# Start of a hybrid decoder trunk: the input is scaled per chunk, the time steps come from the normalised input, and the residual is added by products with the identity

## The chip, the cores and the metric

The kernel runs on one core of a Trainium2 chip. The metric is the device time of one execution in microseconds, the median of the runs. Before the change it is 2892.61 us (2892.17 to 2893.71, three runs).

The engines that matter here: PE (TensorE) multiplies matrices and transposes, DVE (VectorE) and ACT (ScalarE) work elementwise, POOL (GpSimd) works elementwise and issues a few transfers, SP (SyncE) issues most transfers. Each engine works through its own list of instructions in order and waits where an operand is not ready.

## The reference, cut to what matters

A decoder trunk over 1040 tokens (16 learned meta tokens, then 1024 input tokens) of width 1024: a state-space mixer (SSD) and a gated FFN, then attention and a second FFN. All inputs and outputs are float32. The part the change touches is the way into the first mixer and the way out of it.

```python
h = concatenate([meta_tokens, x])                       # 1040 x 1024
u = h * rsqrt(mean(h*h, -1) + 1e-6) * ssd_norm          # _rmsnorm
z, xbc, dt_raw = split(u @ w_in, [2048, 2048 + 3072])   # dt_raw: 32 columns
xbc = silu(causal_conv4(xbc))
dt = softplus(dt_raw + dt_bias);  a = -exp(a_log)
...                                                     # scan over chunks, gate, group norm: hg
h = h + hg @ w_out
```

## The kernel before, in words

**Layout.** Activations lie transposed: 128 features on the partitions, tokens along the free axis, in eight rows (`KD` = 8) of 1040 tokens. Tokens go in three tiles `TT` of 348, 348 and 344. The input comes in nine chunks `CH` of 116 tokens (the last 112), tokens on partitions; three chunks make one tile.

**Products.** A product in nearly full float32 is made of three fp32r products (`mm3`, lines 190 to 195): both operands are split into a high and a low part (`uh`/`ul`, `wh`/`wl`). `parts` (line 295) makes `uh` on ACT (line 303) and `ul` on DVE (line 304); `load_w` (line 171) loads a weight block, makes `wh` on ACT (line 180) and `wl` on POOL (line 98). A plain float32 product is one call and shows as two PE instructions in the trace.

**The way in (`load_x`, lines 327 to 398).** Two steps for each tile j. `stream(j)`: the sum of squares of each chunk (DVE for the chunks in `SQD`, ACT for the others, line 366), then for each of the eight feature blocks three transposes of the raw chunks on PE (`xT`, line 371), a copy into the row `h` (line 374 or 376) and a plain float32 product with the 32 time-step columns of the weights (`dtr`, line 377); then the factors of the tile (`token_rstd`, lines 244 to 250). `scaled(j)`: the three chunks are multiplied by their factors on DVE (line 388), transposed again (`xr`, line 393) and split by `parts`. The rows `h` are stored to the DRAM tensor `h0_d` (line 379) for the residual. All nine chunk loads are issued at the start, the odd chunks on SP's queue, the even ones on ACT's own list, ahead of ACT's other work.

**The mixer.** `mixer` runs `load_x`, then `dt_path` (the softplus of the time steps and their cumulated sums; it multiplies `dtr` by the factors `r9` first), then `in_group(0)`: six blocks of projections (`pj`, 24 products for each tile), with convolution on ACT and DVE. From the first `cb` product (lines 665 and 666) on, the order on PE, DVE, ACT and POOL is fixed by the program (`manual_schedule`) up to the end of the mixer; outside of it a scheduler chooses the order. The last projections of the mixer are interleaved with `split_y` (lines 807 to 815), which scales and splits the first group's gated rows for the output projection: per tile four times DVE, ACT, DVE.

**The way out (`out_proj`, lines 817 to 836).** The groups g = 0, 1, 2 of the output projection run here; the fourth is in `enter_ffn`. For each g and each output block f (eight), `accumulate` (line 424) makes for each of the three token tiles 12 products into one of five PSUM banks (`cycle` over two `mm`, two `lg`, one `ex`) and DVE adds the bank to the row `h[f]` (line 431). With g = 0 the row `h[f]` is first fetched from `h0_d` (line 419).

Of the kernel before, what the change touches and what calls it, by code (L numbers as in the profile page):

```python
# [69 lines left out]
ORD = ((0, 0), (1, 0), (0, 1), (1, 1), (0, 2), (1, 2))  # L70
# [30 lines left out]
class Trunk:  # L101
    def __init__(self, ctx, tc, a):
        self.tc, self.nc, self.a = tc, tc.nc, a
        nc = self.nc
        self.cp = ctx.enter_context(tc.tile_pool(name="cp", bufs=1))
        self.qp = ctx.enter_context(tc.tile_pool(name="qp", bufs=NQ))
        self.tmps = ctx.enter_context(tc.tile_pool(name="up", bufs=8))
        self.wp = ctx.enter_context(tc.tile_pool(name="wp", bufs=3))
        self.mp = ctx.enter_context(tc.tile_pool(name="mp", bufs=2, space=bass.MemoryType.PSUM))
        self.sp = ctx.enter_context(tc.tile_pool(name="sp", bufs=SMB, space=bass.MemoryType.PSUM))  # L110
        self.dp = ctx.enter_context(tc.tile_pool(name="dp", bufs=1, space=bass.MemoryType.DRAM))
        self.n = 0
        self.open = []
        self.consts()
# [56 lines left out]
    def load_w(self, src, n, gain=None, out=None):  # L171
# [8 lines left out]
        nc.scalar.activation(wh[:, :n], w32[:, :n], AF.Copy)  # L180
# [9 lines left out]
    def mm3(self, out, wh, wl, uh, ul, first, last, joins=False, tie=None):  # L190
# [4 lines left out]
        mm(out, wl, uh, start=False, stop=last, skip_group_check=joins)  # L195
# [41 lines left out]
    def token_rstd(self, ss, m, k, eps=EPS, y=None, src=None):  # L237
# [6 lines left out]
        nc.vector.tensor_scalar(ss[:m, :k], (ss if src is None else src)[:m, :k], 1.0 / D, eps, op0=ALU.mult, op1=ALU.add)  # L244
        nc.scalar.activation(y[:m, :k], ss[:m, :k], AF.Ln)
        nc.scalar.activation(y[:m, :k], y[:m, :k], AF.Exp, scale=-0.5)
# [48 lines left out]
    def parts(self, t, u, s0, n, g, eng=None):  # L295
# [6 lines left out]
        else:  # L302
            nc.scalar.activation(h, t, AF.Copy, scale=g)
            nc.vector.scalar_tensor_tensor(l, t, g, h.bitcast(F32), op0=ALU.mult, op1=ALU.subtract)
# [22 lines left out]
    def load_x(self, pool, mx):  # L327
# [5 lines left out]
        wdt = self.wp.tile([P, 1024], F32, tag="w32", name="wdt")  # L333
        self.ln_exp()
        d = self.dp.tile([KD, P, L], F32, tag="h0_d", name="h0_d")
        r9 = mx.tile([P, 3, 3], F32, tag="r9", name="r9")
        dt = self.ex("dtr")
        xs = []
        for c, (t0, n) in enumerate(CH):
# [4 lines left out]
            else:  # L344
                self.by_rows(nc.sync if c % 2 else nc.scalar, xt[:n, :], a["x"][t0 - META : t0 - META + n, :], n)
            if c == 0:
                nc.sync.dma_start(wdt[:, : KD * H], a["w_dt"])
                v = wdt[:, : KD * H].rearrange("p (k h) -> p k h", k=KD)
                nc.gpsimd.tensor_tensor(v, v, self.par("ssd_norm", 0, KD).unsqueeze(2).to_broadcast([P, KD, H]), op=ALU.mult)
# [4 lines left out]
        hs = [self.Q("h") for _ in range(KD)]  # L354

        def stream(j):
            s0, nn = TT[j]
            x3 = xs[3 * j : 3 * j + 3]
            for i in range(3):
                c = 3 * j + i  # L360
                n = CH[c][1]
                t = self.wp.tile([P, D], F32, tag="wl", name=self.nm("junk"))
                if c in SQD:
                    nc.vector.scalar_tensor_tensor(t[:n, :], x3[i][:n, :], 1.0, x3[i][:n, :], op0=ALU.mult, op1=ALU.mult, accum_out=ss[:n, c : c + 1])
                else:
                    nc.scalar.activation(t[:n, :], x3[i][:n, :], AF.Square, accum_out=ss[:n, c : c + 1])
            for k in range(KD):
                ps = self.lg("xT")
                for i in range(3):
                    n = CH[3 * j + i][1]  # L370
                    nc.tensor.transpose(ps[:, i * CB : i * CB + n], x3[i][:n, k * P : k * P + P], self.ident[:n, :n])
                h = hs[k][:, s0 : s0 + nn]
                if k % 2:
                    nc.scalar.activation(h, ps[:, :nn], AF.Copy)
                else:
                    nc.vector.tensor_copy(h, ps[:, :nn])
                nc.tensor.matmul(dt[j * H : j * H + H, :nn], wdt[:, k * H : k * H + H], h, start=k == 0, stop=k == KD - 1)
                if j == 2:
                    nc.sync.dma_start(d[k], hs[k][:, :L])
            self.token_rstd(ss[:, 3 * j : 3 * j + 3], CB, 3, y=r9[:, :, j])  # L380

        def scaled(j):
            s0, nn = TT[j]
            x3 = xs[3 * j : 3 * j + 3]
            for i, t in enumerate(x3):
                n = CH[3 * j + i][1]
                r = r9[:n, i : i + 1, j]
                nc.vector.tensor_scalar(t[:n, :], t[:n, :], r, None, op0=ALU.mult)
            for k in range(KD):
                ps = self.sm("xr")  # L390
                for i in range(3):
                    n = CH[3 * j + i][1]
                    nc.tensor.transpose(ps[:, i * CB : i * CB + n], x3[i][:n, k * P : k * P + P], self.ident[:n, :n])
                self.parts(ps[:, :nn], u[k], s0, nn, self.par("ssd_norm", k))

        for step, j in ORD:
            (scaled if step else stream)(j)
        return d, u, dt, r9
# [35 lines left out]
    def dt_path(self, ps, r9, cp):  # L434
# [3 lines left out]
        heads = cp.tile([P, 2, H], F32, tag="heads", name="heads")  # L438
        nc.gpsimd.dma_start(heads.rearrange("p i h -> p (i h)"), a["heads"].to_broadcast([P, 2 * H]))
        aneg = heads[:, 1]  # L440
        self.tc.keep_in_program_order(nc.scalar.activation(aneg, aneg, AF.Exp))
        nc.vector.tensor_scalar(aneg, aneg, -1.0, None, op0=ALU.mult)
# [17 lines left out]
        tt(v3, pv[R].rearrange("p (c h) -> p c h", h=H), r9[:CB].rearrange("p i j -> p (i j)").unsqueeze(2).to_broadcast([CB, 9, H]), op=ALU.mult)  # L460
        tt(v3, v3, bias, op=ALU.add)
# [41 lines left out]
    def in_block(self, u, col, cv, out):  # L503
# [3 lines left out]
        def tile(w, j):  # L507
# [4 lines left out]
            self.open.append(lambda: nc.scalar.activation(t, t, AF.Silu))  # L512
# [84 lines left out]
    def settle(self):  # L597

        todo, self.open = self.open, []
# [3 lines left out]
    def stream(self, blocks, w0=None):  # L603
# [11 lines left out]
        for n in range(3 * len(todo)):  # L615
            i, j = divmod(n, 3)
            if j == 0:
                if i + 1 < len(todo):
                    w.append(self.load_w(todo[i + 1][0], D))
                cur = w.pop(0)  # L620
            if n in calls:
# [97 lines left out]
    def mixer(self, mx):  # L719


        with self.tc.tile_pool(name="start", bufs=3) as pool:
            hd, u, *dt = self.load_x(pool, mx)
            dt = self.dt_path(*dt, mx)
        with self.tc.tile_pool(name="ssd", bufs=3) as pool:
            yd, rows = [None] * 4, [[] for _ in range(4)]
# [19 lines left out]
            for n, _ in enumerate(self.stream(into(0))):  # L746
# [51 lines left out]
        return hd, rows[3][:4], yd, list(zip(y0[1], y0[0]))  # L798
# [18 lines left out]
    def out_proj(self, hd, y3, yd, ops, pool):  # L817
# [3 lines left out]
        banks = cycle((self.mm, self.lg, self.ex, self.mm, self.lg))  # L821
        for g in range(3):
# [920 lines left out]
    def run(self, ctx):  # L1743
        tc = self.tc
        with tc.tile_pool(name="mx", bufs=1) as mx:
            hd, y3, yd, y0 = self.mixer(mx)
        self.rp = ctx.enter_context(tc.tile_pool(name="rp", bufs=1))
        with tc.tile_pool(name="ff0", bufs=2) as pool:
            d, *forms = self.out_proj(hd, y3, yd, y0, pool)
# [81 lines left out]
```

## Time and profile before

| | |
|---|---|
| median of three runs | 2892.61 us |
| the profiled execution: its time, and the span from its first to its last instruction | 2892.33 us, 2890.5 us |
| DVE busy, ACT busy, POOL busy (share of the span) | 73%, 56%, 56% |
| first product of the projections (`pj`) | at 32.78 us |
| first `cb` product (the scan begins) | at 131.18 us |
| last product of the mixer, first of the output projection | at 645.29 and 645.45 us |

How to read it: a row of the timeline gives the start and the duration in microseconds, the engine, the line, the operation, output and inputs, and the number of instructions merged into it; in brackets stands how long the engine was idle before and what ended that. PE's instructions overlap: a product lasts about 0.32 us, but the next one starts 0.16 us later. So the cost of PE work is read from the distance of the starts. A row of the windows gives for a stretch of time its length, the busy time of each engine with its number of instructions, then the granted TensorE clock, the share of the DMA engines and GB/s.

### The profile page before, as it was taken

Reading aid. Unit: us, or ns where it says so; the run is one execution under the profiler, and the core shown is the slowest. Engines: PE = TensorE matmul, PEld = TensorE weight load, DVE = VectorE, ACT = ScalarE, POOL = GpSimd, SP = SyncE. Lnnn points to the kernel's source line nnn. Section 1 sums busy time; section 2 is a strip of 40 time slices with the busy share of each in tenths; the row PEclk is TensorE's granted clock in tenths of the full one; section 3 lists DMA queues with packets and bytes.
Section 4 is the critical chain, followed back from the end, with each engine's and each line's share of the span. In section 5 each row is a group of like instructions: output and inputs, shape, how many; then the busy total and the mean of one; then the engine's idle time right before and its main releaser. Section 6 shows DMA issues by size and latency. Waiting matters only on the chain. (4 is left out here: it accounts for less than half of the span.)

```text
span 2890.5 us, 58592 instructions
## 1 busy us (share of the span) xinstructions
PE 2834.6 (98%) x21835; PEld 2701.9 (93%) x21835; DVE 2096.3 (73%) x4044; ACT 1628.0 (56%) x3392; POOL 1610.4 (56%) x2430
## 2 busy tenths in 40 slices
PE   7999999999999999999999999999999999999998
PEld 4999999999999999999999999999798999999888
DVE  5676666668387667666886888888749776767776
ACT  4455544544265656565335888888736565555433
POOL 2265555552429888858743222222363888885882
PEclk9999999999999999999999999999999999999999
DMA  5233333343213222244132222222332222225331
GB/s 168 75 107 95 117 94 117 114 156 135 81 60 97 81 81 76 81 161 164 52 114 78 57 68 66 62 63 54 134 117 74 81 76 79 81 81 183 110 102 66
DMA packets 128265, 278.70 MB, mean 96 GB/s; under 512 B 14787, under 2 KB 58828, under 8 KB 127980
## 3 DMA queue, kind: packets, MB, share of 16 engines
q1 hardware_dynamic: 122028, 261.70, 28.7%
q10 hardware_dynamic: 4112, 6.56, 0.7%
q0 software_dynamic: 1840, 6.70, 0.6%
q8 instruction: 172, 2.82, 0.4%
q14 instruction: 113, 0.93, 0.1%
HBM read 204.63 MB, written 55.36 MB: 90 GB/s over the span
## 5 line engine op out<-in xcount | busy, mean ns | idle before, releaser
L98 POOL TENSOR_TENSOR wl<-w,wh 128x256 fp32r<-128x256 f32 x768 | 682.0, 918 | 377.3 <-ACT wh L180 299.8
L193 PE MATMUL pj<-uh,wh 128*128 128x348 f32 (+2 forms) x1536 | 500.0, 326 | 2.7 <-DVE qs L1469 1.9
L194 PE MATMUL pj<-ul,wh 128*128 128x348 f32 (+2 forms) x1536 | 494.7, 322 | 0.0
L195 PE MATMUL pj<-uh,wl 128*128 128x348 f32 (+2 forms) x1536 | 491.5, 320 | 0.0
L193 PE MATMUL p<-bh,fh 128*128 128x262 f32 (+1 forms) x1408 | 400.4, 285 | 5.5 <-DVE p L1118 5.5
L195 PE MATMUL p<-bh,fl 128*128 128x262 f32 (+1 forms) x1408 | 400.1, 284 | 1.9 <-POOL fl L98 1.9
L194 PE MATMUL p<-bl,fh 128*128 128x262 f32 (+1 forms) x1408 | 398.7, 283 | 0.0
L98 POOL TENSOR_TENSOR fl<-x,fh 128x256 fp32r<-128x256 f32 x352 | 265.6, 786 | 191.9 <-ACT fh L1055 161.5
L193 PE MATMUL p<-bh,wh 128*128 128x262 f32 (+1 forms) x1040 | 295.7, 284 | 1.5 <-ACT ft L1115 1.5
L194 PE MATMUL p<-bl,wh 128*128 128x262 f32 (+1 forms) x1040 | 295.8, 284 | 1.2 <-DVE bl L979 1.2
L195 PE MATMUL p<-bh,wl 128*128 128x262 f32 (+1 forms) x1040 | 295.0, 284 | 0.0
L193 PEld LDWEIGHTS pj<-uh,wh 128*128 128x128 f32 x1536 | 288.3, 188 | 5.0 <-issue 1.9
L194 PEld LDWEIGHTS pj<-ul,wh 128*128 128x128 f32 x1536 | 288.9, 188 | 1.1
L195 PEld LDWEIGHTS pj<-uh,wl 128*128 128x128 f32 x1536 | 288.6, 188 | 0.6 <-issue 0.6
L323 DVE SCALAR_TENSOR_TENSOR c<-p,params,c 128x260 f32<-128x260 f32 (+1 forms) x528 | 248.5, 480 | 53.3 <-ACT c L320 46.7
L193 PEld LDWEIGHTS p<-bh,fh 128*128 128x128 f32 x1408 | 267.1, 190 | 6.3 <-DVE p L1118 5.9
L195 PEld LDWEIGHTS p<-bh,fl 128*128 128x128 f32 x1408 | 267.0, 190 | 2.8 <-POOL fl L98 2.5
L194 PEld LDWEIGHTS p<-bl,fh 128*128 128x128 f32 x1408 | 267.5, 190 | 0.1
L1115 ACT ACTIVATE ft<-p 128x262 f32<-128x262 f32 (+1 forms) x352 | 132.5, 382 | 175.0 <-DVE p L1118 111.2
L195 PE MATMUL acc<-gh,wl 128*128 128x260 f32 (+1 forms) x672 | 213.5, 320 | 2.8 <-POOL wl L98 2.6
L193 PE MATMUL acc<-gh,wh 128*128 128x260 f32 (+1 forms) x672 | 210.9, 320 | 3.1 <-DVE h L1279 3.1
L194 PE MATMUL acc<-gl,wh 128*128 128x260 f32 (+1 forms) x672 | 213.9, 319 | 0.0
(332 smaller groups left out, 7898.9 us busy)
## 6 DMA issues: line engine op xcount, KB each, us to landing
w<-in_w_up SPq DMA_DIRECT2D x88, 512.0 KB
w<-in_w_down SPq DMA_DIRECT2D x44, 512.0 KB
w<-in_w_in SPq DMA_DIRECT2D x40, 512.0 KB
E<-ea_d SPq DMA_DIRECT2D x32, 464.0 KB
D<-acs_d SPq DMA_DIRECT2D x32, 420.5 KB
g<-c SPq DMA_DIRECT2D x88, 130.0 KB
g<-c SPq DMA_DIRECT2D x88, 128.0 KB
b<-g SPq DMA_DIRECT2D x16, 520.0 KB
```

Of the source, the lines that this page charges most:

```text
L98: eng.tensor_tensor(out[:, c], x[:, c], y[:, c], op=op)
L193: self.behind(mm(out, wh, uh, start=first, stop=False, skip_group_check=joins), tie, "behind the sums of squares")
L194: mm(out, wh, ul, start=False, stop=False, skip_group_check=joins)
L195: mm(out, wl, uh, start=False, stop=last, skip_group_check=joins)
L323: ins = nc.vector.scalar_tensor_tensor(out, ps[:, o + i : o + i + n], wcol(i), out, op0=ALU.mult, op1=ALU.add)
L1115: nc.scalar.activation(s[:, :N], ps[:, :N], AF.Copy)
```

## The change

Three things.

- **The input is scaled as its chunks land.** The first three chunk loads are issued ahead (chunks 0 and 2 on ACT's list, all others on SP's queue), then the first weight block and the time-step columns, then the other six chunks. Factors are made for two chunks and then for the third of a tile; a chunk is scaled on DVE, on ACT, or half on each. Only the scaled chunks are transposed, once. The squares of the next tile stand between the splits of this one, and ties without a semaphore (`behind`) fix places in the lists.
- **The time steps come from the normalised input.** The 32 columns are split into a high and a low part and laid into zero-padded tiles `wd`, so that a 96-column operand puts the tile's result at its own 32 partitions. `dtr` is now an `mm3` product with `uh`/`ul`: 24 of them, 72 products. They stand behind the projections of the first block for each tile. `dt_path` no longer multiplies by the factors.
- **The residual is added by products.** The rows `h` and the tensor `h0_d` are gone. In `out_proj` with g = 0, `load_rows` loads a column block of the raw input (128 tokens by 128 features, eight pieces, 512 bytes each) and the 16 transposed meta tokens from a small DRAM tensor. The three tiles of a block f are summed first; then `add_rows` adds the input with eleven plain float32 products against the identity (one for the meta tokens, two chunks split at tile borders), and DVE copies the three banks to `h[f]`. The next block starts behind them.

```diff
@@ load_x
+        for c in range(3):
+            load(c)
+        w32 = self.wp.tile([P, 1024], F32, tag="w32", name="w32_0")
+        nc.sync.dma_start(w32, first)
...
+        nc.sync.dma_start(wdt, a["w_dt"])
+        for c in range(3, 9):
+            load(c)
...
+        def transposed(j, ks):
...
+                    t = nc.tensor.transpose(ps[:, i * CB : i * CB + n], x[:n, k * P : k * P + P], self.ident[:n, :n])
+                    if j:
+                        self.behind(t, self.last_mm, "behind the products in front")
+                made[j, k] = self.parts(ps[:, :nn], u[k], s0, nn, self.par("ssd_norm", k))
+
+        def tile(j):
+            a, b, c = range(3 * j, 3 * j + 3)
+            if j == 0:
+                for x in (a, b, c):
+                    square(x, None)
+            factors(j, 0, 2)
+            scale(a, [(nc.vector, 0, D)])
+            factors(j, 2, 1)
+            scale(b, [(nc.scalar if j else nc.vector, 0, D)], None if j else self.first_factor)
...
+            scale(c, [(nc.vector, 0, D // 2), (nc.scalar, D // 2, D)])
+            transposed(j, range(KD // 2))
+            if j < 2:
+                hi, lo = made[j, KD // 2 - 1]
+                square(a + 3, hi)
+                square(b + 3, lo)
+            transposed(j, range(KD // 2, KD))
+            if j < 2:
+                square(c + 3, made[j, KD - 1][0])
...
+        def steps():
+            tile(0)
...
+            yield
+            for j in range(3):
...
+                for k in range(KD):
+                    w = slice(2 * H + G * k - H * j, 2 * H + G * k - H * j + G)
+                    self.mm3(dt[:G, :n], wd[0][:, w], wd[1][:, w], u[k][0][:, c], u[k][1][:, c], j == k == 0, j == 2 and k == KD - 1, tie=self.last_mm)
+                if j < 2:
+                    tile(j + 1)
...
+                yield
@@ add_rows (new)
+            for c in range(SEQ // P):
+                c0 = META + c * P
+                a, b = max(c0, s0), min(c0 + P, s0 + n)
+                if a < b:
+                    own.append((ps[:, a - s0 : b - s0], t[:, c * P : c * P + P], self.ident[:, a - c0 : b - c0]))
+            for i, (out, lhs, rhs) in enumerate(own):
+                ins = mm(out, lhs, rhs, start=False, stop=i == len(own) - 1, skip_group_check=True)
+                self.behind(ins, self.last_mm, "behind the block's products")
+                self.last_mm = ins
+        for (s0, n), ps in zip(TT, banks):
+            self.nc.vector.tensor_copy(t[:, HB + s0 : HB + s0 + n], ps[:, :n])
@@ mixer
+            u, dt, heads, w0, front = self.load_x(pool, mx, self.a["w_in"][DI // P])
+            dt = self.dt_path(dt, heads, mx)
+            next(front)
+            rows = [[] for _ in range(4)]
+            group = self.stream(self.in_group(u, 0, rows[0]), w0, True)
+            for _ in range(3):
+                next(group)
+                next(front)
@@ out_proj
-                    h[f] = self.fetch(hd[f], "h", front=HB)
+                    h[f] = self.load_rows(f)
+                    sums = []
+                    for s0, n in TT:
+                        ps = next(banks)("acc")
+                        for i, (hi, lo) in enumerate(ops):
+                            c = slice(i * P, i * P + P)
+                            self.mm3(ps[:, :n], w[0][:, c], w[1][:, c], hi[:, s0 : s0 + n], lo[:, s0 : s0 + n], i == 0, False, joins=True, tie=tie if i == 0 else None)
+                        sums.append(ps)
+                    self.add_rows(h[f], sums)
+                    tie = self.last_mm
+                    continue
```

The lists of instructions show three places.

ACT's list at the start, before. `x_108`, `x_117`, `x_123`, `x_129`, `x_135` are the even chunks 0 to 8, `junk` is what a sum of squares leaves:

```order
L405 DMA x_108<-in_x 96x1024
L405 DMA x_108<-in_x 4x1024
L405 DMA x_117<-in_x 112x1024
L405 DMA x_117<-in_x 4x1024
L405 DMA x_123<-in_x 112x1024
L405 DMA x_123<-in_x 4x1024
L405 DMA x_129<-in_x 112x1024
L405 DMA x_129<-in_x 4x1024
L405 DMA x_135<-in_x 112x1024
L366 ACTIVATE junk_177,ss_101<-x_108 116x1024
```

And now, where `x_106` and `x_113` are chunks 0 and 2, `mT` the transposed meta tokens and `r` the factors:

```order
L494 DMA x_106<-in_x 96x1024
L494 DMA x_106<-in_x 4x1024
L494 DMA x_113<-in_x 112x1024
L494 DMA x_113<-in_x 4x1024
L375 ACTIVATE junk_190,ss_101<-x_106 116x1024
L431 ACTIVATE mT_186<-mT_177 128x128
L245 ACTIVATE r_104<-ss_101 116x2
L246 ACTIVATE r_104<-r_104 116x2
L375 ACTIVATE junk_194,ss_101<-x_113 116x1024
L245 ACTIVATE r_104<-ss_101 116x1
```

Five of nine chunk loads stood ahead of ACT's first square; now two chunks' loads do, and the square of chunk 2 stands behind the factors of chunks 0 and 1.

DVE's list at the start, now (`x_110` is chunk 1, `tb` a help tile of the factors). Before, the three scalings stood behind all factors of the tile and behind copies of `h`:

```order
L373 SCALAR_TENSOR_TENSOR junk_192,ss_101<-x_110 116x1024
L244 TENSOR_SCALAR ss_101<-ss_101 116x2
L247 TENSOR_TENSOR tb_196<-r_104 116x2
L248 TENSOR_TENSOR tb_196<-tb_196,ss_101 116x2
L249 TENSOR_SCALAR tb_196<-tb_196 116x2
L250 TENSOR_TENSOR r_104<-r_104,tb_196 116x2
L390 TENSOR_SCALAR x_106<-x_106,r_104 116x1024
L244 TENSOR_SCALAR ss_101<-ss_101 116x1
L390 TENSOR_SCALAR x_110<-x_110,r_104 116x1024
```

Then the factors of chunk 2 and its half scaling follow: nothing but this chain stands on DVE ahead of the first split.

PE's list where the output projection begins, before. `acc_6871` is block 0, tile 0; `acc_6885` block 0, tile 1; `acc_6937` block 1, tile 1; `acc_6923` block 1, tile 0:

```order
L195 MATMUL acc_6871<-yh_6669,wl_6864 128x348
L193 MATMUL acc_6885<-yh_6666,wh_6863 128x348
L193 MATMUL acc_6937<-yh_6666,wh_6915 128x348
L194 MATMUL acc_6885<-y_6484,wh_6863 128x348
L195 MATMUL acc_6885<-yh_6666,wl_6864 128x348
L194 MATMUL acc_6937<-y_6484,wh_6915 128x348
L195 MATMUL acc_6937<-yh_6666,wl_6916 128x348
L193 MATMUL acc_6923<-yh_6666,wh_6915 128x348
```

And now, from the end of block 0, tile 2 (`acc_6852`) to the first product of block 1 (`acc_6890`); `ms` are sums of squares of the last gate group, `h_6823` the loaded input:

```order
L195 MATMUL acc_6852<-yh_6624,wl_6819 128x344
L482 MATMUL acc_6826<-h_6823,ident 128x16
L482 MATMUL acc_6826<-ident,h_6823 128x128 x2
L482 MATMUL acc_6826<-ident,h_6823 128x76
L482 MATMUL acc_6839<-ident,h_6823 128x52
L226 MATMUL ms_6780<-z_6224,ones 128x348
L482 MATMUL acc_6839<-ident,h_6823 128x128 x2
L226 MATMUL ms_6794<-z_6261,ones 128x344
L482 MATMUL acc_6839<-ident,h_6823 128x40
L482 MATMUL acc_6852<-ident,h_6823 128x88
L482 MATMUL acc_6852<-ident,h_6823 128x128 x2
L193 MATMUL acc_6890<-yh_6621,wh_6882 128x348
```

Before, PE took blocks 0, 1 and 2 in turns, whichever token tile was ready; now block 1 begins only when all three tiles of block 0 and its eleven identity products are through.

More of the change, by code (lines that the diff above doesn't have):

```diff
@@ L382, in scaled @@
[L382 to L394, printed above, removed]
@@ L396, in load_x, with square @@
-        for step, j in ORD:
-            (scaled if step else stream)(j)
-        return d, u, dt, r9
+        G = 3 * H
+        wd = [self.Q("wd", F32R) for _ in range(2)]
+        for t in wd:
+            nc.gpsimd.memset(t.bitcast(F32), 0.0)
+        taps = [t[:, 2 * H : 2 * H + KD * G].rearrange("p (k h) -> p k h", h=G)[:, :, :H] for t in wd]
+        made = {}
+        def square(c, tie):
+            n = CH[c][1]
+            t = self.wp.tile([P, D], F32, tag="wl", name=self.nm("junk"))
+            x, acc = xs[c][:n, :], ss[:n, c : c + 1]
+            if c in SQD:
+                ins = nc.vector.scalar_tensor_tensor(t[:n, :], x, 1.0, x, op0=ALU.mult, op1=ALU.mult, accum_out=acc)
+            else:
+                ins = nc.scalar.activation(t[:n, :], x, AF.Square, accum_out=acc)
+            self.behind(ins, tie, "behind the tile in front")
@@ L601, in settle, with stream @@
             f()
-    def stream(self, blocks, w0=None):
+    def stream(self, blocks, w0=None, late=False):
         calls = {}
@@ L797, in mixer @@
                     pass
[L798 removed]
+        return rows[3][:4], yd, list(zip(y0[1], y0[0]))
     def fetch_y(self, d):
```

137 lines of the change are left out of this document (79 added, 58 removed).

## The prediction

> **What bounds the kernel now.** I read the page first, then the windows of the mixer, then the timeline at the two places that the change touches: the start and the beginning of the output projection.
>
> ```profile
> span 2890.5 us, 58592 instructions
> PE 2834.6 (98%) x21835; PEld 2701.9 (93%) x21835; DVE 2096.3 (73%) x4044; ACT 1628.0 (56%) x3392; POOL 1610.4 (56%) x2430
> 131.00:645.30 514.30, 511.52 (x3845) 478.17 (x3844) 342.86 (x820) 267.51 (x393) 293.78 (x398) 1.00 0.37 109
> ```
>
> PE is busy 98% of the span. In the third row, from the first `cb` product to the last product of the mixer (length, then busy time of PE, weight loads, DVE, ACT, POOL), PE works 511.52 of 514.30 us at clock 1.00. The change leaves PE's list of that stretch as it is, so whatever the front gains or loses reaches 645.3 nearly whole, and whatever PE pays after it stands in the span. I therefore count PE time at the two ends and every wait of PE there.
>
> ```profile
> 0.84 14.41 ACTq L405 DMA_DIRECT2D x<-in_x  x9
> 11.35 1.01 PE L371 MATMUL xT<-ident,x 116*128 116x116 f32 x4 [4.95 <-DMA x<-in_x]
> 12.64 1.22 DVE L364 SCALAR_TENSOR_TENSOR junk<-x 116x1024 f32<-116x1024 f32 x1
> 15.36 1.06 ACT L366 ACTIVATE junk<-x 116x1024 f32<-116x1024 f32 x1 [13.27 <-DMA x<-in_x]
> 17.58 0.17 DVE L244 TENSOR_SCALAR ss<-ss 116x3 f32<-116x3 f32 x1 [0.41 <-ACT junk L366]
> 18.83 0.19 ACT L245 ACTIVATE r<-ss 116x3 f32<-116x3 f32 x1
> 19.05 0.21 ACT L246 ACTIVATE r<-r 116x3 f32<-116x3 f32 x1
> 19.29 0.16 DVE L247 TENSOR_TENSOR tb<-r 116x3 f32<-116x3 f32 x1 [1.55 <-ACT r L246]
> 26.55 3.56 DVE L388 TENSOR_SCALAR x<-x,r 116x1024 f32<-116x1024 f32 x3
> 28.72 0.83 PE L393 MATMUL xr<-ident,x 116*128 116x116 f32 x6
> 32.78 0.40 PE L193 MATMUL pj<-uh,wh 128*128 128x352 f32 x1
> 131.18 0.27 PE L665 MATMUL cb<-ident,xbc 128*116 128x128 f32 x1
> ```
>
> The front: chunks 0 and 1 are there at 11.35 (what PE's 4.95 us wait ends on), but ACT issues loads until 15.25 and squares only at 15.36, and the scalings wait until 26.55 behind the copies of `h`. From 28.6 to 131.0 PE works on, first partly cold.
>
> **The front: what PE sheds.**
>
> ```profile
> 33.25 0.77 PE L377 MATMUL dtr<-h,wdt 128*32 128x348 f32 x2
> 33.96 0.52 PE L371 MATMUL xT<-ident,x 116*128 116x116 f32 x3
> 34.31 0.46 PE L393 MATMUL xr<-ident,x 116*128 116x116 f32 x3
> 34.54 0.41 PE L194 MATMUL pj<-ul,wh 128*128 128x352 f32 x1
> 130.85 0.32 PE L194 MATMUL pj<-ul,wh 128*128 128x352 f32 x1
> 131.01 0.33 PE L195 MATMUL pj<-uh,wl 128*128 128x352 f32 x1
> ```
>
> By the distance of starts a `dtr` pair costs 33.96-33.25, less queueing some 0.67; a group of `xT` 0.35; a `pj` 0.16. By the lists, 8 of 24 `dtr` and 10 of 24 `xT` groups are behind PE at 28.6. Of the 102.4 us up to 131.0, 16×0.67 = 10.7 are `dtr`, 14×0.35 = 4.9 `xT`; 86.8 are common to both kernels (456 `pj` = 73.0, 24 `xr` groups at some 0.3 = 7.4, about 1.5 of small work, which leaves 4.9 of waits).
>
> **The front: when PE starts now.** Chunks 0 and 1 at about 11.0; square 1.22, its handoff and the small operation of line 244 to 12.5; Ln and Exp (0.19, 0.21) with handoffs to 13.0; four small DVE operations of 0.16 to 13.8; scaling, 3.56/3 = 1.19 at most (a scaling is 0.93 in the mean, below) to 14.8; line 244 and the second scaling to 15.9; four small ones to 16.7; half a scaling: first complete `xr` group at 17.1, first `pj` near 18. Bounds for the start are 16 (no handoff waits) and 19 (scalings all at 1.19, and chunk 2 late).
>
> **The front: what PE takes on.** 72 `dtr` products at 0.16 = 11.5. And each tile now is paced by its splits:
>
> ```profile
> L303 ACT ACTIVATE uh<-xr,params 128x348 fp32r<-128x348 f32 x16 | 8.3, 548 | 8.2 <-PE xr L393 8.2
> L304 DVE SCALAR_TENSOR_TENSOR ul<-xr,params,uh 128x348 fp32r<-128x348 f32 x16 | 8.8, 572 | 3.3 <-ACT uh L303 3.3
> L388 DVE TENSOR_SCALAR x<-x,r 116x1024 f32<-116x1024 f32 x8 | 7.2, 932 | 1.8 <-PE xT L371 1.8
> ```
>
> Eight splits (4.6), one square (1.2), a scaling (0.9) and the factors (1.0) make 7.7 on DVE; PE has 24 products and 8 groups of transposes, 6.3, beside it: 1.4 of wait for each tile, 4.2. With 2.5 for cold products at the start and 0.7 of handoffs that is 7.4, of which 4.9 stand in the common part: +2.5 (bounds -3, if squares and scalings hide wholly, and +7, if tiles 1 and 2 wait once more for their factors). First `cb`: 17.1 + 86.8 + 11.5 + 2.5 = **117.9**, a gain of **13.1** (bounds 8.5 and 16.5; 20.5 if PE never waited). `dt_path` keeps 123 `pj`, 19.6 us, between its sums and the first `cb`, and hides there.
>
> **The output projection: identity products.**
>
> ```profile
> 131.29 0.36 PE L666 MATMUL cb<-xbc,xbc 128*116 128x116 f32 x2
> 131.49 0.60 PE L669 MATMUL px<-ident,xbc 128*116 128x128 f32 x4
> 131.84 0.41 PE L193 MATMUL pj<-uh,wh 128*128 128x352 f32 x1
> 662.67 1.32 PE L226 MATMUL ms<-z,ones 128*128 128x348 f32 x4
> ```
>
> The nearest row is a plain float32 product of 116 columns: 131.49-131.29 = 0.20, 1.72 ns a column. A block's eleven cover 1040 columns: 1.79, and 0.26 for short ones whose weight load shows: 2.05, times eight **16.4**. From below: a transpose against the identity takes (131.84-131.49)/4 = 0.088 for 128 columns, 0.72 a block, 5.7 in all; from above, line 226 at 1.82 ns a column and every weight load bare, 20.
>
> **The output projection: a new stall.**
>
> ```profile
> 645.29 0.32 PE L195 MATMUL pj<-uh,wl 128*128 128x344 f32 x1
> 645.45 0.32 PE L193 MATMUL acc<-yh,wh 128*128 128x348 f32 x1
> 648.82 0.42 PE L193 MATMUL acc<-yh,wh 128*128 128x348 f32 x1 [0.37 <-DVE h L431]
> 658.11 0.52 DVE L815 TENSOR_TENSOR y<-t,yh 128x344 fp32r<-128x344 f32 x1
> 659.67 0.52 DVE L815 TENSOR_TENSOR y<-t,yh 128x344 fp32r<-128x344 f32 x1 [0.56 <-ACT yh L814]
> 694.33 0.32 PE L193 MATMUL acc<-yh,wh 128*128 128x348 f32 x1
> ```
>
> `split_y` paces by 1.57 us (658.11 to 659.67) through DVE, ACT, DVE, and ends at 660.2. Before, PE filled that time with blocks 1 and 2 on the tiles at hand. Now it may not: after tile 0 (1.9) it gets three products per 1.57. The chain doesn't get faster: the adds of line 431 that go stood in its gaps. In old time block 0 ends at 660.2 + 0.47 (last three products) + 2.05 + 1.28 (two `ms` that the list puts in between, by the row of line 226) = 664.0; without waits at 645.45 + 36×0.159 (the distance of starts there) + 2.05 + 1.28 = 654.5. Of the 9.5 some 1.5 is not new: short waits that the old order had (0.37 shown) and slow single products after them. **8.0**, at least 7.3 if the chain gains half a step, at most 9.5.
>
> Does the stall also cool the clock?
>
> ```profile
> 852.81 0.39 PE L193 MATMUL p<-bh,fh 128*128 128x262 f32 x1 [1.86 <-DVE p L1118]
> 854.00:856.00 2.00, 2.00 (x11) 2.00 (x11) 2.00 (x7) 2.00 (x7) 0.00 (x0) 0.50 0.00 0
> 856.00:858.00 2.00, 2.00 (x14) 2.00 (x14) 2.00 (x7) 1.57 (x4) 0.00 (x0) 0.71 0.03 8
> ```
>
> After thin work and an idle of 1.86 us the granted clock (third column from the end) falls to 0.50 and 0.71: half speed for some 3.4 us, 1.7 lost. The new stall is of that kind, some eight gaps of 1.1 us: I add **1.7** (0 to 3.4). The Trainium skill ("TensorE: Matmul & The Clock Gate", Part 1, on the oscillation of the clock gate) warns of idle gaps longer than about 3.4 us; by it gaps of 1.1 would cost no clock. The trace does not quite agree: an idle of 1.86 stands ahead of the slow clock, though in thin work.
>
> Blocks 1 to 7 then take 36×0.159 + 2.05 = 7.77 each, 54.4. So g = 1 starts at 664.0 + 54.4 + 1.7 = 720.1 against 694.33: **+25.8**.
>
> **What costs nothing.**
>
> ```profile
> 642.21 3.72 SPq L419 DMA_DIRECT2D h<-h_d  x8
> E<-ea_d SPq DMA_DIRECT2D x32, 464.0 KB
> 595.00:596.00 1.00, 1.00 (x8) 1.00 (x7) 1.00 (x5) 0.98 (x4) 0.90 (x2) 1.00 1.09 348
> ```
>
> The fetch of `h` (first row) becomes a load of 0.52 MB per block in 512-byte pieces. The second row's transfers, in 464-byte pieces, ran in the window of the third, at 348 GB/s (its last column); all eight blocks, 4.2 MB, are then about 14 us behind issues that stand at the same place, and block f is needed only at 660 + 7.8f. If a block came at half that rate it would be in time too; a late first one is rival D. The copies of a bank on DVE cost what the adds of line 431 did. Three of five banks are held per block; the next block's third bank waits for a copy of 0.5 us issued some 5 us before. DVE's list behind the copies holds the splits of g = 1, with POOL and ACT half idle; they are ready before 720.
>
> **Sum.** The three terms behind the mixer make 26.1, the starts of g = 1 give 25.8 (the old stretch had a little more waiting); I keep the latter: 25.8 - 13.1 = **+12.7**: span 2903.2, execution 2892.33 + 12.7 = 2905.0, and the median of the runs shown stands 0.3 above the profiled execution: **2905**.
>
> **The rivals.**
>
> A, not slower: the identity products run at the transposes' price, since they have the same operand and shape (0.088 per 128 columns). It decides once a block's eleven cost under 1.1 us; at 0.72 it gives -13.1 + 5.7 + 8.0 + 1.7 = +2.3, 2895. Against it: the only plain float32 row, 0.20 for 116, is an ordinary product, as these are. 7%.
>
> B, no new stall: PE's blocks run late enough, or `split_y` early enough, that its chain ends before PE asks. -13.1 + 16.4 = +3.3, 2896. For it: nothing but slack in front, as DVE is busy 73%. Against: the chain's last step at 659.67 is 14 us after PE arrives, and both move together with the front. 6%.
>
> C, the front gains less: chunks, 4.2 MB behind one queue, or the first weight block land late, or PE runs cold through tile 0, so that `pj` start at 22. Gain 8.5: +17, 2910. For it: PE's first products before were cold too (the `pj` at 32.78 shows 0.40). 15%.
>
> D, the first block's rows come late: SP's list holds weights between them, and 512-byte pieces are the smallest of the way. 5 to 6 us more of waiting at 660: +18, 2911. 9%.
>
> E, the change doesn't do what it says: the first factors come no earlier, since the chain still waits for the same two chunks, and the front gains nothing: +25.8, 2918. Against it: 15.36 and 26.55 have causes that go. 3%.
>
> F, faster: the front gains 16.5, A's price is half reached (1.1 a block, 8.8) and the stall is filled: -7.7, 2885. It needs three things at once: 5%.
>
> G, the clock stays at 1.00 through the stall: for it, single short waits (0.37 above) left it so before; against it, the row with 0.50. +11.0, 2903.6. The page on the clock gate named above says this one. 17%.
>
> **How the numbers follow.** My forecast has 38%, G 17%: both are the same course with and without one term. What a measurement can tell is 0.2%, 5.8 us. F is faster: 5%. A and B lie within the bound: 13%. Forecast, G, C, D and E are slower: 82%. The range: below, A and B at 2895 and 2896; above, C and D at 2910 and 2911, and 1 for later blocks of the FFN, whose order shifts a little: 2895 to 2912. The forecast's own range, by the bounds of the gain (±4) and of the identity products (±3.5), is 2900 to 2910.
>
> **What would show it.** Right: the first square on ACT before 12 us, first `xr` at 17, first `pj` near 18, first `cb` at 118; PE gaps of about 1.1 us between triples of `acc` for some 13 us after the mixer, a clock under 1.00 behind them, line 482 with some 2 us per block, and 75 us from the mixer's last product to g = 1 (49 before). Wrong: a first `cb` after 122 (C); line 482 under 1.1 us per block (A); no gaps (B); PE waiting on a DMA at line 482 (D). The forecast falls altogether if the stretch from the first `cb` to the mixer's end isn't 514 us any more, or if PE waits anew in the gated FFN.

## The result and the profile after

| | before | after |
|---|---|---|
| median (lowest to highest; runs) | 2892.39 us (2889.38 to 2893.71; 4) | 2910.01 us (2908.71 to 2911.49; 4) |
| ratio, 95% interval | | 1.0063 (1.0045 to 1.0080) |
| span of the profiled execution | 2890.5 us | 2909.3 us |
| first `cb` product | 131.18 | 116.00 |
| last product of the mixer | 645.29 | 630.41 |
| first product of the gated FFN (`p`) | 839.67 | 855.60 |

17.6 us slower by the medians, 18.8 by the profiled executions, where 12.7 were forecast. The page after:

```profile
span 2909.3 us, 58877 instructions
PE 2847.2 (98%) x21971; PEld 2730.0 (94%) x21971; DVE 2083.2 (72%) x4044; ACT 1630.7 (56%) x3393; POOL 1616.0 (56%) x2432
```

PE is as full as before, so the stages are compared one by one. The windows of the stages (length, busy time of PE, weight loads, DVE, ACT, POOL, then the granted clock), of the kernel before:

```profile
28.72:131.18 102.46, 100.41 (x615) 87.51 (x614) 61.36 (x117) 50.55 (x88) 21.36 (x30) 1.00 0.35 113
645.29:839.67 194.38, 193.77 (x1298) 191.05 (x1296) 134.80 (x280) 74.00 (x153) 73.37 (x97) 1.00 0.33 111
```

and of the changed one:

```profile
15.38:116.00 100.62, 97.79 (x604) 94.75 (x605) 56.78 (x121) 56.29 (x102) 23.51 (x34) 1.00 0.31 88
116.00:630.41 514.41, 511.54 (x3842) 478.02 (x3841) 343.89 (x823) 268.11 (x395) 292.45 (x392) 1.00 0.37 110
630.41:855.60 225.19, 218.41 (x1474) 213.75 (x1472) 133.33 (x280) 75.12 (x153) 74.70 (x103) 0.97 0.32 97
```

The mixer's stretch is the same within 0.3 us (514.41 against 645.29 - 131.18 = 514.11). The way in, up to its end, is 645.29 - 630.41 = 14.9 us shorter. The way out, from the mixer's last product to the first of the FFN, is 225.19 - 194.38 = 30.8 us longer, and in it PE idles 225.19 - 218.41 = 6.8 us, where it idled 0.6. The rest of the span grows by 2.9 (2909.3 - 855.60 against 2890.5 - 839.67). -14.9 + 30.8 + 2.9 = 18.8.

The timeline of the changed kernel's start:

```profile
5.39 1.06 ACT L375 ACTIVATE junk<-x 116x1024 f32<-116x1024 f32 x1 [3.31 <-DMA x<-in_x]
7.56 1.23 DVE L373 SCALAR_TENSOR_TENSOR junk<-x 116x1024 f32<-116x1024 f32 x1 [6.41 <-DMA x<-in_x]
12.16 1.06 ACT L375 ACTIVATE junk<-x 116x1024 f32<-116x1024 f32 x1 [2.61 <-DMA x<-in_x]
14.84 0.48 DVE L390 TENSOR_SCALAR x<-x,r 116x512 f32<-116x512 f32 x1
15.38 0.84 PE L400 MATMUL xr<-ident,x 116*128 116x116 f32 x3 [0.33 <-DVE x L390]
16.48 0.66 PE L193 MATMUL pj<-uh,wh 128*128 128x352 f32 x1 [0.25 <-ACT uh L303]
```

ACT's first square runs at 5.39 where it ran at 15.36; each square waits for its own chunk. What comes last is the third chunk (chunk 2), at 12.16, and from it the chain runs to the first complete `xr` group at 15.38 and the first `pj` at 16.48 (28.72 and 32.78 before).

The beginning of the output projection, where the bracket gives PE's idle time and what ended it:

```profile
630.41 0.32 PE L195 MATMUL pj<-uh,wl 128*128 128x344 f32 x1
634.05 0.42 PE L193 MATMUL acc<-yh,wh 128*128 128x348 f32 x1 [0.92 <-ACT yh L907]
637.19 0.66 PE L193 MATMUL acc<-yh,wh 128*128 128x348 f32 x1 [0.30 <-ACT yh L907]
644.44 0.44 ACT L628 ACTIVATE z<-pj 128x344 f32<-128x344 f32 x1
644.93 0.66 PE L193 MATMUL acc<-yh,wh 128*128 128x344 f32 x1 [4.87 <-ACT z L628]
648.54 0.44 PE L482 MATMUL acc<-h,ident 128*128 128x16 f32 x2
...
658.62 0.29 PE L482 MATMUL acc<-h,ident 128*128 128x16 f32 x2
658.76 2.48 PE L482 MATMUL acc<-ident,h 128*128 128x128 f32 x20
660.99 0.40 PE L193 MATMUL acc<-yh,wh 128*128 128x348 f32 x1
```

Two things are to be seen. The second tile's products come in threes behind the splits, as forecast. But the third tile (344 tokens) doesn't follow its splits: PE stands for 4.87 us until ACT has read the bank that the mixer's last projection filled (line 628), and on ACT that read stands behind the last split. And a block's identity products take 660.99 - 658.62 = 2.37 us. The clock in that stretch (third column from the end):

```profile
634.00:636.00 2.00, 1.39 (x4) 1.00 1.11 280
636.00:638.00 2.00, 1.57 (x5) 0.62 1.17 296
638.00:640.00 2.00, 2.00 (x4) 0.50 1.08 308
...
648.00:650.00 2.00, 2.00 (x11) 0.50 0.71 287
650.00:652.00 2.00, 2.00 (x13) 0.97 0.05 14
```

By the first and the last of these rows the clock falls to half at about 636.5 and is back at about 650.1.

At the start of the FFN one more piece shows (two waits of PE in the timeline):

```profile
880.34 0.59 PE L193 MATMUL p<-bh,fh 128*128 128x262 f32 x1 [1.11 <-ACT fh L1159]
883.45 0.59 PE L195 MATMUL p<-bh,fl 128*128 128x262 f32 x1 [1.87 <-POOL fl L97]
```

and in the window around them, at half clock:

```profile
880.00:886.00 6.00, 3.79 (x15) 3.49 (x16) 6.00 (x16) 2.26 (x6) 5.63 (x5) 0.50 0.25 87
```

Here the scheduler, whose choice depends on everything ahead, has put other products first: of the first 1000 `p` products 78 stand elsewhere in PE's list than before. The first 300 take 50.4 us from the first one, against 45.4 before.

### The profile page after: what moved, and what is told of

The parts are those of the page before. It is cut to its first block, busy times and chain, and to the rows that moved or that the text cites. A ratio compares the mean times of both kernels' runs of the same rounds, so it can differ in the third digit from the quotient of the medians.

```text
span 2909.3 us, 58877 instructions
## 1 busy us (share of the span) xinstructions
PE 2847.2 (98%) x21971; PEld 2730.0 (94%) x21971; DVE 2083.2 (72%) x4044; ACT 1630.7 (56%) x3393; POOL 1616.0 (56%) x2432
```

## The experiments

The table gives for each kernel the medians, and from its profiled execution the mixer's last product, the stretch from there to the FFN's first product, and the rest of the span. The runs were made in four groups; the kernel before ran beside each, with medians from 2891.2 to 2892.4.

| kernel | median | ratio to before (interval) | mixer ends | stretch | rest |
|---|---|---|---|---|---|
| before | 2892.4 | | 645.29 | 194.4 | 2050.8 |
| changed | 2910.0 | 1.0063 (1.0045 to 1.0080) | 630.41 | 225.2 | 2053.7 |
| e1, no identity products | 2887.5 | 0.9983 (0.9974 to 0.9993) | 630.88 | 205.4 | 2049.5 |
| e2, other banks | 2910.2 | 1.0062 (1.0047 to 1.0077) | 630.54 | 223.8 | 2054.4 |
| e3, by tiles, no tie | 2892.2 | 1.0001 (0.9992 to 1.0010) | 630.93 | 212.9 | 2048.4 |
| e4, transposed input at g = 0 | 2900.6 | 1.0034 (1.0022 to 1.0045) | 629.11 | 214.6 | 2053.1 |
| e6, products alone | 2919.6 | 1.0093 (1.0078 to 1.0108) | 643.59 | 225.0 | 2046.7 |
| e8, transposed input at g = 1 | 2883.9 | 0.9972 (0.9961 to 0.9983) | 629.80 | 202.4 | 2047.6 |
| e9, no tie, at the block's end | 2908.1 | 1.0055 (1.0040 to 1.0070) | 631.03 | 222.6 | 2055.7 |
| e10, by tiles, tied | 2904.4 | 1.0041 (1.0026 to 1.0056) | 631.09 | 223.9 | 2048.3 |
| f1, chunk loads on ACT | 2914.6 | 1.0081 (1.0066 to 1.0095) | 638.83 | 225.3 | 2049.3 |
| e8, run again beside f2 | 2884.4 | 0.9977 (0.9968 to 0.9986) | 629.78 | 202.6 | 2055.0 |
| f2, e8 with PE kept warm | 2882.5 | 0.9971 (0.9961 to 0.9981) | 628.16 | 201.6 | 2047.7 |

The last column scatters between 2046.7 and 2055.7 with no edit in that part of the code. The scheduler orders a few dozen products there otherwise in some kernels; but one and the same kernel scatters as much, e8 with 2047.6 in one execution and 2055.0 in the other. A part of the change is therefore read from its own stretch, and the median only beside it.

**e1: what the identity products cost.**

```diff
-            for i, (out, lhs, rhs) in enumerate(own):
-                ins = mm(out, lhs, rhs, start=False, stop=i == len(own) - 1, skip_group_check=True)
-                self.behind(ins, self.last_mm, "behind the block's products")
-                self.last_mm = ins
...
```

The residual is missing from the sums; the last product of a tile ends its sum instead of the last identity product.

> The changed kernel without the 88 identity products (the residual is left out of the sums; its loads, the order of the blocks and the copies stay). If the products lie bare on PE at the 2.37 us a block that the changed kernel's trace shows: 8 x 2.37 = 19 us less, 2891. If PE would wait anyway at their places (for copies to free the banks, or for weights): 5 us less or nothing, 2905 to 2910.

The stretch falls from 225.2 to 205.4: 19.8 us, the bare price of 8 x 2.37 = 19.0 and a little for those of block 0, which run at half clock. The median falls by 22.5, 3 more; in the profile the rest of the span is 4.2 shorter, which is within that column's scatter. The stall stays: the windows still hold 205.36 - 198.88 = 6.5 us of idle PE.

```profile
630.88:836.24 205.36, 198.88 (x1297) 194.00 (x1296) 134.35 (x280) 74.52 (x153) 75.82 (x103) 0.97 0.35 107
```

**e2: the bank.**

```diff
-        banks = cycle((self.mm, self.lg, self.ex, self.mm, self.lg))
+        banks = cycle((self.mm, self.lg, self.mm, self.lg, self.ex))
```

> The changed kernel with the banks of the output projection taken in another turn, so that block 0's third tile goes to one of the two mm banks and not to the single ex bank. If the 4.87 us wait ahead of that tile is for the ex bank, which ACT reads (line 628) only behind the last split: the wait becomes four short ones that follow the splits, block 0 ends 2 to 3 us earlier, 2907.5. If the tile waits for its operands: no change, 2910.

The 4.87 us wait is gone, so it was for the bank. In its place, in e2's timeline, the third tile follows its splits at a distance of 1.56 us, at half clock:

```profile
640.03 0.66 PE L193 MATMUL acc<-yh,wh 128*128 128x344 f32 x1
...
641.59 0.65 PE L193 MATMUL acc<-yh,wh 128*128 128x344 f32 x1
...
644.71 0.66 PE L193 MATMUL acc<-yh,wh 128*128 128x344 f32 x1
...
646.00 0.44 PE L482 MATMUL acc<-h,ident 128*128 128x16 f32 x2
646.28 3.69 PE L482 MATMUL acc<-ident,h 128*128 128x128 f32 x16
```

The tile ends at 646.00 where it ended at 648.54, as expected; but now nearly all identity products of the block run at half clock, until about 650, and the stretch gains 1.4 us. The median gains nothing, where 2.5 were expected: the rest of the span is 0.7 longer in the one profile, and the intervals don't separate the two.

**e3, e9 and e10: the tie, the place, or both.** The changed kernel puts the identity products at the block's end and ties the next block behind them. e3 undoes both, e9 the tie alone, e10 the place alone:

```diff
 e3 and e10
-                        sums.append(ps)
-                    self.add_rows(h[f], sums)
-                    tie = self.last_mm
+                        self.add_rows((rows, h[f]), ps, s0, n)
...
 e10 alone, behind it
+                    tie = self.last_mm
 e9 (against the changed kernel)
-                    tie = self.last_mm
```

> The changed kernel with the identity products of a tile right behind that tile's products, its copy behind them, and no tie between the blocks. If the new stall comes from the tie: PE fills it with other blocks as before the change, the clock stays at 1.00, and of the 79.5 us between the mixer and g = 1 there stay 49 + 19 = 68: 2898.5. If the splits or the banks hold PE whatever the order: less than 3 us gained, 2907 or more.

> The changed kernel without the tie that puts a block behind the identity products of the block in front; the identity products stay at the end of the block. The lists let two tiles of block 1 (3.8 us of products) into the stall, but block 0's third tile still waits for the ex bank. If the tie makes the stall: 3.8 us and some cold time less, 2905. If the place of the identity products makes it: no change, 2910.

> The kernel of e3 (identity products and copy right behind each tile) with the tie put back, so that a block starts behind the identity products of the block in front. If the tie makes the stall, it is back: the products of the first two tiles (0.8 us each) fall into it, 2908. If the place of the identity products made it: near e3, 2892 to 2895.

With both gone the stall is gone. e3's windows have PE full, at clock 1.00:

```profile
640.00:644.00 4.00, 4.00 (x31) 3.79 (x30) 3.19 (x8) 1.48 (x3) 0.00 (x0) 1.00 1.07 263
630.93:843.83 212.90, 212.90 (x1473) 211.12 (x1472) 136.12 (x280) 74.52 (x153) 73.83 (x100) 1.00 0.34 102
```

The stretch falls by 12.3 us to 212.9, as expected; what remains over before, 18.5, is identity products: PE works 212.90 - 193.77 = 19.1 us longer than before and no longer waits. The median fell by 17.8, more than the 11.5 expected; in the profiles 5.3 of it is the rest of the span. With one of the two gone it hardly moves: 222.6 in e9, 223.9 in e10. Both wait for the same bank (e9's row, then e10's):

```profile
645.57 0.43 PE L193 MATMUL acc<-yh,wh 128*128 128x344 f32 x1 [4.02 <-ACT z L628]
```

```profile
645.60 0.65 PE L193 MATMUL acc<-yh,wh 128*128 128x344 f32 x1 [3.38 <-ACT z L625]
```

So neither theory as I put them for e9 and e10 holds. Without the tie, three banks are still held until the block's third tile is through, and PE, in order, stands at it after two tiles of block 1 (48 products of four tiles run from 631.19 on in e9, then the wait). With the tie but by tiles, there is nothing else to do. A stretch of 212.9 needs both: banks given back tile by tile, and a list that may run ahead to other blocks.

**e6: do front and residual add up?** The kernel before, with its own front, and the changed kernel's output projection (`load_rows`, `add_rows`, the tie); of the stores to DRAM only the meta columns stay.

```diff
-                if j == 2:
-                    nc.sync.dma_start(d[k], hs[k][:, :L])
+                if j == 0:
+                    nc.sync.dma_start(d[k], hs[k][:, :META])
...
```

> The kernel before with the third part of the change alone: its own front (the rows h still feed the time steps, of the stores only the meta columns are left), and the output projection of the changed kernel. If front and residual add up: the 30.8 us that the changed kernel's trace shows more between the mixer's last product and the first FFN product come on top of 2892.2, so 2923, 2 or 3 more if the FFN's first tiles are reordered too. If part of the loss is a collision that only the earlier front brings: 2915 or less.

The stretch is 225.0, that of the changed kernel: the loss doesn't depend on the front. The mixer ends 1.7 us earlier; the stores are all that the edit takes from the front. The median stands 27.3 above before, between the two expectations and less than the 30.8: beside those 1.7, the rest of the span is 4.1 shorter in its profile.

**f1: what the front's gain comes from.** Chunks 4, 6 and 8 are loaded from ACT's list again.

```diff
-                self.by_rows(nc.scalar if c == 2 else nc.sync, xt[:n, :], a["x"][t0 - META : t0 - META + n, :], n)
+                self.by_rows(nc.sync if c % 2 else nc.scalar, xt[:n, :], a["x"][t0 - META : t0 - META + n, :], n)
```

> The changed kernel with one piece of its front undone: chunks 4, 6 and 8 are loaded from ACT's list again, ahead of ACT's first square, as in the kernel before. If the front's gain comes from ACT's list coming free (first square at 5.39 in place of 15.36): the square is back at about 15, the first pj 9 us later, 2919. If it comes from scaling by chunks and from fewer PE instructions: no more than 2 us, 2910 to 2912.

f1's timeline:

```profile
17.13 1.05 ACT L375 ACTIVATE junk<-x 116x1024 f32<-116x1024 f32 x1
25.18 0.66 PE L193 MATMUL pj<-uh,wh 128*128 128x352 f32 x1 [0.25 <-ACT uh L303]
```

The first square waits until ACT has issued its loads (from 0.83 to 16.91 us in f1's trace), the first `pj` comes 8.7 us later, and the mixer ends 8.4 later. So of the front's 14.9 us, 8.4 hang on three loads in ACT's list. The median rose by 4.6 only, where 9 were expected: in the profile the rest of the span is 4.4 shorter than in the changed kernel.

**e4 and e8: the residual without identity products.** Both load the same rows, transpose them on PE (8 a block, no accumulation) and leave the sums to DVE. In e4 ACT copies them to `h` at g = 0 and the sums are added as before the change; in e8 DVE copies the sums at g = 0 and adds the input at g = 1:

```diff
 e8
...
+        for c0 in range(0, SEQ, 4 * P):
+            ps = self.sm("xt")
+            for i in range(4):
+                nc.tensor.transpose(ps[:, i * P : i * P + P], x[:, c0 + i * P : c0 + i * P + P], self.ident)
+            o = slice(HB + META + c0, HB + META + c0 + 4 * P)
+            nc.vector.tensor_tensor(h[:, o], h[:, o], ps[:, : 4 * P], op=ALU.add)
...
```

> The changed kernel's front, but the residual as before in the output projection (h plus sums on DVE, no tie), where h comes from 8 transposes of the loaded rows for each block on PE and two copies on ACT. If identity products and stall are the whole loss: 64 transposes at 0.09 = 6 us in place of 30.5, 2910 - 24.5 = 2885.5, faster than both. If the transposes' copies on ACT delay the splits or the adds wait for them: 2895 or more.

> The changed kernel's front; in the output projection each tile's sums are copied to h at g = 0 with no tie (blocks in turns as in the kernel before), and the input is added at g = 1: 8 transposes of the loaded rows on PE for each block, and DVE adds them from PSUM. If identity products and stall are the whole loss and the front's 14.9 us are real: 64 transposes at 0.09 take 5.7, so 2892.2 - 14.9 + 5.7 = 2883. If the adds hold up DVE at g = 1, or the waits come back elsewhere: 2890 or more.

e4 missed by 15 us: it keeps 20 of the 31 us. At g = 0 its adds need the transposed rows, the list has the first transposes behind the third tile of block 0, which waits for the ex bank there too, and they wait in turn for banks of their own (e4's timeline):

```profile
649.61 0.66 PE L471 MATMUL xt<-ident,x 128*128 128x128 f32 x4 [1.08 <-DVE z L232]
652.81 1.11 PE L471 MATMUL xt<-ident,x 128*128 128x128 f32 x4 [2.54 <-ACT h L473]
```

e8 takes this need away from g = 0. PE's list there is like that of before, and the transposes stand at g = 1, eight in 693.44 - 692.65 = 0.79 us:

```profile
692.65 1.03 PE L468 MATMUL xt<-ident,x 128*128 128x128 f32 x8
693.44 0.41 PE L193 MATMUL acc<-yh,wh 128*128 128x348 f32 x1
```

Its stretch is 202.4, 8.0 over before: 64 transposes at 0.1 and 1.6 of waits. 2883.9, as expected, and faster than both kernels; a second time, beside f2, 2884.4, ratio 0.9977 (0.9968 to 0.9986).

> The kernel of e8 again, for the comparison with the next on the same chip: 2884, and under the kernel before beyond the interval.

**f2: the cold start.** e8 with 26 products of the identity with itself on PE while it waits for the first chunks.

```diff
+        warm = self.ex("warm")
+        for i in range(26):
+            self.warm = nc.tensor.matmul(warm[:, :P], self.ident, self.ident, start=True, stop=True)
...
```

> The kernel of e8 with 26 products of the identity with itself on PE between 5.7 and about 14 us, while PE waits for the first scaled chunks; nothing reads them. If the clock of 0.50 from the first pj on (0.29 us from start to start until 22 us) costs time: the pj start at 0.16, 3 us less than e8, 2881. If the splits pace the first tile anyway: the same as e8.

f2's timeline:

```profile
5.61 8.85 PE L434 MATMUL warm<-ident 128*128 128x128 f32 x52
16.81 0.43 PE L193 MATMUL pj<-uh,wh 128*128 128x352 f32 x1
...
17.95 0.32 PE L195 MATMUL pj<-uh,wl 128*128 128x352 f32 x1
18.11 0.33 PE L193 MATMUL pj<-uh,wh 128*128 128x352 f32 x1
```

The products now start 0.16 us apart, and the mixer ends at 628.16, 1.6 us ahead of e8. That is half of the 3 expected. The 3 had been read from the changed kernel, which is cold (at the wider distance of 0.29) until 22 us; e8's first execution is at 0.16 from about 20 us on. From the first `pj` to the first `cb` f2 takes 113.73 - 16.81 = 96.9 us, e8 98.6 and 99.4 in its two executions, the changed kernel 116.00 - 16.48 = 99.5: a cold start costs 1.7 to 2.6 us here, by how long it lasts. The medians, 2882.5 and 2884.4, lie that way, but their intervals overlap: shown in the profile, open in the time.

## Why the prediction was right, and where its terms were off

**The direction and the range held**, for the reason given: the mixer's stretch passes a shift through (514.41 against 514.11), the front gains, the output projection loses twice as much. That the sum came within 5 us is in part luck: the front's gain was larger than forecast, and took back 1.8 of the 7.9 by which the losses were larger (5.0 on the way out, 2.9 in the rest). And 2910.0 stands at the upper end of the forecast's own range, 2900 to 2910; the 2 us above it had been allowed for C, D and the later FFN, and neither C nor D happened.

**The front: 13.1 forecast, 14.9 measured.** From the first complete `xr` group to the first `cb` 100.8 us were forecast (86.8 + 11.5 + 2.5) and 100.6 came, so shed work, added work and extra waits were right as a sum. Of its terms two can be read: 2.5 for cold products, where f2 gives 2.6 (99.5 against 96.9), and 4.9 for waits, where PE idles 100.62 - 97.79 = 2.8 in all; the others were not measured singly. The start was off: 17.1 against 15.38. I let chunks 0 and 1 land at 11.0 and the chain hang on them; they were squared from 5.39 (on ACT) and 7.56 (on DVE), and the last to come of the three, chunk 2 at 12.16, made the end. That the `pj` at 32.78 was cold, as I read from its 0.40 in rival C, does not follow: in f2, where PE was kept warm, the first `pj` lasts 0.43. That the gain comes from ACT's list is shown by f1 for 8.4 of the 14.9; how the rest is shared between chunk-wise factors and the cheaper time steps was not tried.

**The identity products: 16.4 forecast, 19.8 by e1, 18.5 by e3.** The step that failed is "0.26 for short ones whose weight load shows". I scaled the long ones by columns, but a pair of instructions of 16 columns takes 658.76 - 658.62 = 0.14, where columns alone give 0.03: the short products cost more than by their columns, and five of the eleven are shorter than 128. By 2.37 a block the eleven take 0.58 more than the 1.79 of their columns, not 0.26. Rival A, the transposes' price, is out: 2.37 a block, not under 1.1.

**The stall: 8.0 + 1.7 forecast, 12.3 by e3.** Against e3, which has the same products, the changed kernel's stretch holds 6.8 us of waiting and 218.41 - 212.90 = 5.5 us more busy time. So the waiting was near its 8.0, and what was mis-sized is the 1.7 for the slow clock. Of the stall's cause two steps fell. First, I named the tie alone. It is the tie or the block's end, and only without both does it go (e9, e10). Second, I let the third tile follow its splits. It waited instead for a bank, behind a read that stands after the last split on ACT; I had counted banks among what costs nothing, and looked only at banks that blocks of the output projection hold, not at the one that the mixer leaves. Taking that wait away (e2) moved the stretch by 1.4 us, since the splits' pace stood right behind it.

**The cold clock.** 1.7, at most 3.4, was taken from a row with 3.4 us at half speed; here it was 13.6 us (636.5 to 650.1), some 5 of which PE idled anyway. The other 8.5 us at half speed lose about 4, by estimate: most of the 5.5 above. Rival G is out. The Trainium skill ("TensorE: Matmul & The Clock Gate", Part 1) has the clock fall after an idle window of about 3.4 us. In this trace it fell to 0.62 in the window from 636 to 638, when no gap had been longer than the 0.92 at 634.05; the wait of 4.87 came later. Nor does the longest gap decide it. In e10 the clock fell between 636 and 640 after gaps of at most 0.44; in e9, with one of 0.49 at 634.67, it stayed at 1.00 until after its wait of 4.02 (e9's window, then e10's):

```profile
636.00:640.00 4.00, 3.76 (x20) 3.05 (x20) 2.98 (x6) 1.41 (x4) 0.00 (x0) 1.00 1.15 299
```

```profile
636.00:640.00 4.00, 3.15 (x10) 2.35 (x11) 2.97 (x6) 1.45 (x4) 0.00 (x0) 0.74 1.18 299
```

So several short gaps were enough here; how much idle time it takes, these runs do not show.

**The rest of the span.** I allowed 1 us for it, and wrote that the forecast falls altogether if PE waits anew in the gated FFN. The changed kernel's profile has such waits: 5.0 us within the first 300 `p` products, around 880, and 2.9 over the whole rest. The other terms can be read all the same, but this sign of being wrong did come. In every other kernel run here these products take 45.4 or 45.5 us, in those too that have the same output projection (e6 and f1), so it is not a cost of the residual. That the scheduler's order makes it is likely, as only this kernel has that order there, but was not tried: the changed kernel has one profile, and e8's second execution shows a wait of 3.04 us a little later that its first does not have.

Rivals B to F: the stall was there (B); the first `cb` came at 116.00 (C); PE never waited for a load at line 482 (D); the front came earlier (E); and the gain was 14.9, not more than the loss (F).

## What to carry to other kernels

Adding a residual by products with the identity is not free work: on a full PE it costs its products, here 18.5 to 19.8 us, where transposing the same rows once and adding them on an engine with room (DVE, busy 145 of 202 us in e8) costs 8. A fixed order that makes the next block wait for the whole of this one takes away the work that used to fill the gaps; look at what PE would run while the operands of the block still arrive, and which bank the next tile needs and who reads it last. And put a small sum where nothing waits for it: the same transposes cost 20 us at g = 0, where the sums need them, and 8 at g = 1.

## What the runs showed that was not expected

The clock column can show 1.00 for a cold PE. At the changed kernel's start it shows 1.00 from 16 to 22 us, while `pj` products start 0.29 us apart (18.05 to 18.34) and 0.16 only from 22.30 on; in f2, with PE at work before, they start 0.16 apart at once. The trace holds no record of the granted clock before 22.07 us in the changed kernel, and none before 11.46 in f2; without a record the column shows 1.00. The distance of the starts tells more there. The timeline, then one of the windows:

```profile
18.05 0.49 PE L195 MATMUL pj<-uh,wl 128*128 128x352 f32 x1
18.34 0.49 PE L193 MATMUL pj<-uh,wh 128*128 128x352 f32 x1
...
22.30 0.32 PE L195 MATMUL pj<-uh,wl 128*128 128x352 f32 x1
22.46 0.32 PE L193 MATMUL pj<-uh,wh 128*128 128x352 f32 x1
```

```profile
18.00:20.00 2.00, 2.00 (x9) 1.00 1.04 268
```
